# Output projections, norms and residual by tokens, in two staggered halves

## The chip, the cores and the metric

The kernel runs on one core of one Trainium2 chip. A core has five engines that run side by side, each through its own instructions in order: TensorE (PE; its weight loads are listed apart, as PEld), VectorE (DVE), ScalarE (ACT), GpSimd (POOL) and SyncE (SP), which here issues the transfers. They hand work to each other through semaphores. The metric is the device time of one execution in microseconds (us).

## The reference

Two layers over 256 latent tokens with 256 context tokens beside them, 1024 channels, float32. Each layer is a half-step feed-forward block, a token mixer, and a second half-step feed-forward block. In front of each stands a normalization with shift and scale, behind it a second one with a gate, and the result is added to the stream. The vectors for shift, scale and gate come from a conditioning vector times `w_mod`.

```python
def pre(x, m, k, g):
    return rms_norm(x, g) * (1 + m[:, 3 * k + 1, None]) + m[:, 3 * k, None]
def post(y, m, k, g):
    return m[:, 3 * k + 2, None] * rms_norm(y, g)
def swiglu(h, w_gu, w_down):
    gt, up = jnp.split(h @ w_gu, 2, axis=-1)
    return (jax.nn.silu(gt) * up) @ w_down
...
        x_lat = x_lat + FFN_RES * post(swiglu(pre(x_lat, m_lat, 0, g[0]), ff1_w_gu[i], ff1_w_down[i]), m_lat, 0, g[1])
```

`rms_norm` divides each token by the root of the mean square of its channels. The mixer of layer 0 is a gated depthwise convolution (31 taps) beside an attention with 8 heads, in which latent queries read a window of the latent grid and all context keys; that of layer 1 is a short gated convolution. The context is needed only up to the keys and values of layer 0. The feed-forward width is 2816.

## The kernel before

All activations lie with channels on the partitions and tokens along the free dimension: a stage's input is 8 tiles of 128 channels by 256 tokens (512 in ff1_0, where latent and context tokens run side by side). The stages follow one another: ff1_0, ev_in, ev_out, ff2_0 (layer 0), ff1_1, od_in, od_out, ff2_1 (layer 1).

Weights stream from memory in 162 chunks of 1 MB, each 16 tiles of 128x128, through SP's queue. A chunk is cut into four pieces of 128x512. ScalarE rounds a piece (`wh`, L190) and VectorE takes the rest (`wl`, L192); activations are split in the same way. Every product is three matmuls (`mm3`, L202 to L206): the weights are the stationary operand, the activations move, 256 columns at a time in the latent stages, 512 in ff1_0. Only the V projection (L624 to L626) has it the other way round.

A norm sums over channels, hence over partitions. `Post.tile` (L250) squares each output tile as it comes; `Post.rstd` (L266) sums over partitions by matmuls with a constant matrix (L271, L284), takes the power -1/2 on GpSimd (`power`, L214), and spreads the result over all partitions by matmuls with the identity (`spread`, L220). The mean square of the new stream is worked out from three sums, so that both powers need only one pass. Then `step` updates x (L308, L309) and builds the next input tile by tile (`pre_tile`, L226 to L237); the next stage's first matmuls run over its tiles for four output tiles at a time.

ff1_0 has four parts of 5, 5, 6 and 6 of the 22 hidden tiles; after each the down projection of that part is added up in `yp`. Products of `silu(c)` with `w_mod` run on VectorE as 1024-wide dot products (L126) in the background of ff1_0 and ff2_0; their rows are loaded as `mr` on SP's queue between the weights.

A scheduler sets the order of the instructions on each engine from the order of the program and the dependencies; the engines keep that order. Tile pools set how far ahead things may run: 3 weight chunks, 8 pieces of `wh` and of `wl`, and eight PSUM banks, four for products.

## Time and profile before

| | us |
|---|---|
| three runs | 1269.46, 1271.57, 1272.31 |
| median | 1271.57 |
| span of the profiled execution | 1270.2 |
| TensorE busy in it | 1228.3 (97%) |
| VectorE, ScalarE busy | 951.7 (75%), 632.8 (50%) |

The span runs from the first to the last instruction of one profiled execution. Busy time of TensorE counts matmuls from issue to modelled end, so the rate of a stream is read from the number of matmuls in a stretch, and a stop of the stream from the gap between two issues.

### The profile page before, as it was taken

How to read it: one execution, taken by the hardware profiler on the slowest of the kernel's cores; microseconds unless marked ns; L12 is line 12 of the kernel's file. 1: busy time of each engine (PE TensorE's matmuls, PEld its weight loads, DVE VectorE, ACT ScalarE, POOL GpSimd, SP SyncE). 2: the span in 40 equal slices, each digit the busy share in tenths (PEclk: the TensorE clock that was granted, in tenths of full speed). 3: DMA queues.
4: the chain of work that ended last, by engine and by line, in shares of the span. 5: the costliest groups of instructions: out<-in, count | busy, mean ns of one | idle time of the engine just before them, and what ended most of it. 6: DMA issues, size and time to landing. Idle time of an engine off the chain costs nothing.

```text
span 1270.2 us, 21721 instructions
## 1 busy us (share of the span) xinstructions
PE 1228.3 (97%) x8338; PEld 1125.4 (89%) x8338; DVE 951.7 (75%) x1919; ACT 632.8 (50%) x1262; POOL 16.6 (1%) x25
## 2 busy tenths in 40 slices
PE   7999999999999999989999999999998998999996
PEld 4688888888888986689999999999998998999996
DVE  4999998886358999877988868565667777755553
ACT  4543322322346746667555547555555555655551
POOL 0000000000000000000000000000000000000000
PEclk8999999999999999999999998999999998999998
DMA  8757788887221420126888944545453543554541
GB/s 305 298 198 268 285 309 324 296 295 277 100 83 50 167 100 34 67 100 229 350 320 331 348 180 138 195 174 192 177 188 118 189 176 116 202 196 170 196 167 34
DMA packets 37455, 252.22 MB, mean 199 GB/s; under 512 B 3940, under 2 KB 7140, under 8 KB 7144
## 3 DMA queue, kind: packets, MB, share of 16 engines
q1 hardware_dynamic: 37352, 250.85, 53.3%
q8 instruction: 65, 1.06, 0.3%
q14 instruction: 38, 0.31, 0.1%
HBM read 249.78 MB, written 1.05 MB: 197 GB/s over the span
## 4 chain that ended last, share of the span: by engine, by line
PE 85%; DVE 8%; DMA 3%; ACT 2%; issue 1%; POOL 1%; SPq 0%; POOLq 0%; DVEq 0%; ACTq 0%
PE mm L205 26%; PE mm L206 26%; PE mm L204 26%; DMA mr<-in_wmodb 2%; DVE bufD L567 2%; DVE junk L126 2%; DVE wl L192 1%; PE bc L668 1%; PE mm L647 1%; PE st L677 1%; DVE acc L262 1%; DMA xlc<-in_ctxT 1%; PE bc L220 1%; PE mm L625 0%; PE mm L626 0%
## 5 line engine op out<-in xcount | busy, mean ns | idle before, releaser
L190 ACT CAST wh<-wr 128x512 fp32r<-128x512 f32 x648 | 399.5, 622 | 467.0 <-PE mm L205 422.7
L192 DVE TENSOR_TENSOR wl<-wr,wh 128x512 fp32r<-128x512 f32 x648 | 442.0, 688 | 205.1 <-ACT wh L190 202.7
L205 PE MATMUL mm<-hin,wh 128*128 128x256 f32 x1248 | 355.4, 286 | 0.1
L206 PE MATMUL mm<-hin,wl 128*128 128x256 f32 x1248 | 355.2, 286 | 0.0
L204 PE MATMUL mm<-hin,wh 128*128 128x256 f32 x1248 | 350.7, 286 | 4.6 <-ACT hin L233 4.6
L204 PEld LDWEIGHTS mm<-hin,wh 128*128 128x128 f32 x1248 | 240.1, 195 | 5.5 <-ACT hin L233 5.5
L205 PEld LDWEIGHTS mm<-hin,wh 128*128 128x128 f32 x1248 | 243.3, 195 | 0.3 <-DVE hin L237 0.3
L206 PEld LDWEIGHTS mm<-hin,wl 128*128 128x128 f32 x1248 | 243.1, 195 | 0.0
L126 DVE SCALAR_TENSOR_TENSOR junk<-mr,cb 128x1024 bf16<-128x1024 f32 x156 | 190.3, 1220 | 8.9 <-DMA mr<-in_wmodb 8.2
L204 PE MATMUL mm<-hh,wh 128*128 128x512 f32 (+1 forms) x464 | 170.1, 371 | 2.0 <-ACT hh L427 1.3
L205 PE MATMUL mm<-hl,wh 128*128 128x512 f32 (+1 forms) x464 | 171.7, 371 | 0.0
L206 PE MATMUL mm<-hh,wl 128*128 128x512 f32 (+1 forms) x464 | 171.1, 370 | 0.4 <-DVE wl L192 0.4
L204 PEld LDWEIGHTS mm<-hh,wh 128*128 128x128 f32 x464 | 87.6, 190 | 17.6 <-ACT hh L427 1.8
L206 PEld LDWEIGHTS mm<-hh,wl 128*128 128x128 f32 x464 | 88.3, 190 | 15.2 <-DVE wl L192 0.8
L205 PEld LDWEIGHTS mm<-hl,wh 128*128 128x128 f32 x464 | 88.4, 190 | 14.8 <-DVE hl L237 0.2
L204 PE MATMUL mm<-Hc,wh 128*128 128x256 f32 x288 | 81.5, 283 | 0.0
L205 PE MATMUL mm<-Hd,wh 128*128 128x256 f32 x288 | 81.5, 283 | 0.0
L206 PE MATMUL mm<-Hc,wl 128*128 128x256 f32 x288 | 81.5, 283 | 0.0
L205 PE MATMUL mm<-Hl,wh 128*128 128x512 f32 (+1 forms) x182 | 69.8, 383 | 0.5 <-DVE Hl L326 0.5
L206 PE MATMUL mm<-Hh,wl 128*128 128x512 f32 (+1 forms) x182 | 69.5, 382 | 0.0
L204 PE MATMUL mm<-Hh,wh 128*128 128x512 f32 (+1 forms) x182 | 69.4, 382 | 0.0
L206 PEld LDWEIGHTS mm<-Hc,wl 128*128 128x128 f32 x288 | 55.2, 192 | 0.0
(217 smaller groups left out, 1701.9 us busy)
## 6 DMA issues: line engine op xcount, KB each, us to landing
wr<-in_wflow SPq DMA_DIRECT2D x162, 1024.0 KB, 4.8
mr<-in_wmodb SPq DMA_DIRECT2D x64, 1024.0 KB, 6.5
mr<-in_wmoda SPq DMA_DIRECT2D x4, 1024.0 KB, 8.7
wme<-in_wmoda SPq DMA_DIRECT2D x4, 1024.0 KB, 4.8
bt<-in_bias SPq DMA_DIRECT2D x2, 1024.0 KB, 5.6
xlc<-in_xT SPq DMA_DIRECT2D x2, 512.0 KB, 6.0
xlc<-in_ctxT SPq DMA_DIRECT2D x2, 512.0 KB, 8.1
out<-xlc SPq DMA_DIRECT2D x3, 256.0 KB, 2.6
```

The costliest lines, as they stand in the source:

```text
L126: nc.vector.scalar_tensor_tensor(junk, row, 1.0, cb[:, v, :], op0=ALU.mult, op1=ALU.mult, accum_out=mraw[:, l, v, ch, j:j + 1])
L190: nc.scalar.copy(h, r)
L192: nc.vector.tensor_sub(lo, r, h.bitcast(F32))
L204: nc.tensor.matmul(ps, lhsT=wh, rhs=xh, start=start, stop=False, skip_group_check=check)
L205: nc.tensor.matmul(ps, lhsT=wh, rhs=xlo, start=False, stop=False, skip_group_check=check)
L206: nc.tensor.matmul(ps, lhsT=wl, rhs=xh, start=False, stop=stop, skip_group_check=check)
L220: nc.tensor.matmul(bc[:, t * P:(t + 1) * P], lhsT=r[:, t:t + 1].to_broadcast([P, P]), rhs=ident, start=True, stop=True)
L262: nc.vector.tensor_add(self.acc, self.acc, s)
L567: nc.vector.scalar_tensor_tensor(acc[:, i, :], src, dwh[:, i, d:d + 1], acc[:, i, :], op0=ALU.mult, op1=ALU.add)
L647: nc.tensor.matmul(ps, lhsT=qT[rows, i, t * P:(t + 1) * P], rhs=kT[rows, i, :], start=True, stop=True)
L668: nc.tensor.matmul(pt[:, kt * P:(kt + 1) * P], lhsT=pr[:, kt * P:(kt + 1) * P], rhs=dg, start=True, stop=True)
L677: nc.tensor.matmul(po[m * DH:(m + 1) * DH, :S], lhsT=vv[:, kt, h * DH:(h + 1) * DH], rhs=pTs[:, m, kt, :], start=(kt == 0), stop=(kt == 3))
```

## The change

The output projections (FFN down, ev_out, od_out) now have the activations stationary and 512 weight columns moving (`rows3`), so that their outputs lie with tokens on the partitions: two token halves of 128, each in two banks of 512 channels. In `Out` all but the last four k-tiles run for both halves; the last four run first for half 0 and then for half 1. Each half has its own norm: `residual` squares on ScalarE with the sum along the row, multiplies by the gate, which now lies as a row on all partitions (`gate_row`, by way of memory on GpSimd's queue), takes the power on GpSimd, updates x, which now lies by tokens (`xt`), and squares x again for the second power. `turn` scales x, transposes it on TensorE (8 transposes of 128x128 a half) and applies shift and scale. The next FFN's first two hidden tiles (the head) are computed by tokens and by halves (`head_mm`) and transposed (`head_turn`); the other twenty stay as before. The 2 MB of x and context by tokens are loaded by an extra transfer. The weights come in halves of a chunk (5 buffers), with 12 pieces ahead; modulation rows in 512 KB, 4 buffers; six PSUM banks hold products. ff1_0 has five parts of 4, 4, 4, 5 and 5. The K projection runs as two times 256 columns. The output is stored by tokens.

```diff
-TAIL = ((0, 2), (2, 2), (4, 2), (6, 1), (7, 1))
+HEAD = 2
+TAIL = 4
...
-PARTS0 = (5, 5, 6, 6)
-BG0 = (4, 1)
+PARTS0 = (4, 4, 4, 5, 5)
+BG0 = (4, 2)
...
+RING = 12
+RAW = CHUNK // 2
...
+    def gate_row(l, v, k, res):
+        p = mod_post(l, v, k, res)
+        flat = dram.tile([KD, P], F32, name=f"prow{l}{v}{k}")
+        nc.gpsimd.dma_start(out=flat.rearrange("k p -> p k"), in_=p)
+        row = mraw_p.tile([P, D], F32, name="pr", tag="mr")
+        nc.gpsimd.dma_start(out=row, in_=flat.rearrange("k p -> (k p)").partition_broadcast(P))
+        return row
...
+    def load(n, m):
+        if (n, m) not in raws:
+            raws[n, m] = wraw.tile([P, RAW], F32, name="wr")
+            nc.sync.dma_start(out=raws[n, m], in_=wflow[n][:, m * RAW:(m + 1) * RAW])
+        return raws[n, m]
...
+    def rstd(ss):
+        u = small.tile([P, 1], F32, name="uu")
+        nc.vector.scalar_tensor_tensor(u, ss[:, 0:1], EPS, ss[:, 1:2], op0=ALU.add, op1=ALU.add)
+        r = small.tile([P, 1], F32, name="rr1")
+        nc.gpsimd.tensor_tensor(r, u, nhalf[:, :1], op=ALU.pow)
+        return r
+    def square(ss, n, y):
+        nc.scalar.activation(ajunk, y, AF.Square, scale=1.0 / 32, accum_out=ss[:, n:n + 1])
...
+    def residual(y, row, x, yw, out_t=None):
+        ss = small.tile([P, 2], F32, name="ss")
+        for n in range(2):
+            c = slice(n * 512, (n + 1) * 512)
+            square(ss, n, y[n])
+            nc.vector.tensor_mul(yw[:, c], y[n], row[:, c])
+        r = rstd(ss)
+        s2 = small.tile([P, 2], F32, name="s2")
+        for n in range(2):
+            c = slice(n * 512, (n + 1) * 512)
+            nc.vector.scalar_tensor_tensor(x[:, c], yw[:, c], r, x[:, c], op0=ALU.mult, op1=ALU.add)
+            if out_t is None:
+                square(s2, n, x[:, c])
+            else:
+                nc.sync.dma_start(out=out_t[:, c], in_=x[:, c])
+        return rstd(s2) if out_t is None else None
...
+    def turn(x, rx, xs, a, b, h, t):
+        ts = slice(t * P, (t + 1) * P)
+        for n in range(2):
+            c = slice(n * 512, (n + 1) * 512)
+            nc.scalar.activation(xs[:, c], x[:, c], AF.Copy, scale=rx)
+            pt = bank(ps_bc, "bc")
+            for q in range(4):
+                nc.tensor.transpose(pt[:, q * P:(q + 1) * P], xs[:, n * 512 + q * P:n * 512 + (q + 1) * P], ident)
+            full = work.tile([P, 512], F32, name="gh")
+            for q in range(4):
+                k = 4 * n + q
+                nc.vector.tensor_scalar(full[:, q * P:(q + 1) * P], pt[:, q * P:(q + 1) * P], a[:, k:k + 1],
+                                        b[:, k:k + 1], op0=ALU.mult, op1=ALU.add)
+            fv = full.rearrange("p (q t) -> p q t", t=P)
+            nc.scalar.copy(h[:, 0, 4 * n:4 * n + 4, ts], fv)
+            nc.vector.tensor_sub(h[:, 1, 4 * n:4 * n + 4, ts], fv, h[:, 0, 4 * n:4 * n + 4, ts].bitcast(F32))
...
+    def rows3(ps, src, k, ts, w, start, stop):
+        wh, wl = w
+        nc.tensor.matmul(ps, lhsT=src[:, 0, ts], rhs=wh, start=start, stop=False)
+        nc.tensor.matmul(ps, lhsT=src[:, 0, ts], rhs=wl, start=False, stop=False)
+        nc.tensor.matmul(ps, lhsT=src[:, 1, ts], rhs=wh, start=False, stop=stop)
...
+    class Out:
+        def __init__(self, name, base, src, K, row, final=False):
+            w = lambda k, n: wtile(name, base + k * KD + n * 4, 4)
+            y = [[bank(ps_mm, "mm") for _ in range(2)] for _ in range(2)]
+            tmp = big.tile([P, 4, D], F32, name="tmp", tag="E")
+            self.xs = [tmp[:, 2 + t, :] for t in range(2)]
+            self.rx = []
+            for k in range(K - TAIL):
+                for t in range(2):
+                    for n in range(2):
+                        rows3(y[t][n], src(k), k, TS[t], w(k, n), k == 0, False)
             for t in range(2):
...
+                for n in range(2):
+                    for k in range(K - TAIL, K):
+                        rows3(y[t][n], src(k), k, TS[t], w(k, n), False, k == K - 1)
+                self.rx.append(residual(y[t], row, xt[:, t, :], tmp[:, t, :], out[t] if final else None))
...
+    def half_step(prev, name, l, k, final=False, nbg=0):
+        a, b = mod_pre(l, 0, k)
+        hin = lat_in()
...
+        def head_mm(t):
+            ps = bank(ps_mm, "mm")
+            for kk in range(KD):
+                rows3(ps, hin[:, :, kk, :], kk, TS[t], wtile(name, 4 * kk, 4), kk == 0, kk == KD - 1)
...
+        prev.turn(0, a, b, hin)
+        head_mm(0)
+        prev.turn(1, a, b, hin)
+        head_mm(1)
...
+            if f == HEAD:
+                head_turn(0)
+                head_turn(1)
+            gate_up(H(f)[:, 0, :], H(f)[:, 1, :], ps[:, :S], ps[:, S:], S)
...
+        row = gate_row(l, 0, k, 0.5)
+        bg(nbg)
+        return Out(name, NF * 16, H, NF, row, final)
...
+    xt = big.tile([P, 4, D], F32, name="xt", tag="X")
+    nc.sync.dma_start(out=xt, in_=xtok)
...
+            def turn0(t):
+                turn(xt[:, t, :], rxs[t], yp[:, t, :], *pre[t // 2], hs[t // 2], t % 2)
+        for t in range(4):
+            ts = slice(t * P, (t + 1) * P)
+            y = [bank(ps_mm, "mm") for _ in range(2)]
+            for n in range(2):
                 for k in range(nf):
...
+                    wh, wl = wtile("ff1_0", base + k * KD + n * 4, 4)
+                    nc.tensor.matmul(y[n], lhsT=Hh0[:, k, ts], rhs=wh, start=k == 0, stop=False)
+                    nc.tensor.matmul(y[n], lhsT=Hh0[:, k, ts], rhs=wl, start=False, stop=False)
+                    nc.tensor.matmul(y[n], lhsT=Hl0[:, k, ts], rhs=wh, start=False, stop=k == nf - 1)
+            for n in range(2):
+                c = slice(n * 512, (n + 1) * 512)
+                if pi == 0:
+                    nc.scalar.copy(yp[:, t, c], y[n])
+                else:
+                    nc.vector.tensor_add(yp[:, t, c], y[n], yp[:, t, c])
+            if last:
+                rxs.append(residual([yp[:, t, :512], yp[:, t, 512:]], prow[t // 2], xt[:, t, :], yp[:, t, :]))
+                if t >= 2:
+                    turn0(t - 2)
...
+    turn0(2)
+    turn0(3)
...
+            for v in range(2):
+                mm3(ps[:, v * S:(v + 1) * S], wtile("ev_in", 128 + i * KD + k), hs[v][:, 0, k, :], hs[v][:, 1, k, :],
+                    k == 0 and v == 0, k == KD - 1, True)
...
+    post = Out("ev_out", 0, lambda k: mix[:, :, EV_ORDER[k], :], KD, gate_row(0, 0, 1, 1.0))
+    post = half_step(post, "ff2_0", 0, 2, nbg=BG1)
...
+    hin = lat_in()
+    post.turn(0, a, b, hin)
+    post.turn(1, a, b, hin)
```

In the fences below the order on one engine is shown, of the program before and of the one after, an instruction a row with its line, kind, output and inputs. First VectorE between ff2_0 and ff1_1. Before (L282 and L274 sums, L300 to L297 the small vectors of the norm, L308 and L309 the update of x, L226 the input):

```order
L282 TENSOR_TENSOR sq_7525<-sq_7525,acc 128x256
L274 TENSOR_SCALAR uu<-st 128x2
L282 TENSOR_TENSOR sq_7525<-sq_7525,acc 128x256
L300 COPY rc_7593<-rr 128x2
L288 COPY xy<-mm 128x2
L292 SCALAR_TENSOR_TENSOR q_7584<-st,rr,xy 128x1 x2
L295 SCALAR_TENSOR_TENSOR sx<-q_7584,rr,sx 128x1 x2
L308 TENSOR_TENSOR xn<-yg,bc 128x256
L297 TENSOR_SCALAR sx<-sx 128x2
L309 TENSOR_TENSOR xlc<-xlc,xn 128x256
L226 TENSOR_TENSOR xn<-xlc,bc 128x256
```

After (L243 the gate product, L229 the sum in front of a power, L248 the update of x, L267 shift and scale, L194 a weight split):

```order
L243 TENSOR_TENSOR tmp<-mm,pr 128x512 x2
L229 SCALAR_TENSOR_TENSOR uu<-ss 128x1
L194 TENSOR_TENSOR wl<-wr,wh 128x512
L248 SCALAR_TENSOR_TENSOR xt<-tmp,rr_7234,xt 128x512 x2
L194 TENSOR_TENSOR wl<-wr,wh 128x512 x3
L229 SCALAR_TENSOR_TENSOR uu<-s_7236 128x1
L194 TENSOR_TENSOR wl<-wr,wh 128x512 x2
L243 TENSOR_TENSOR tmp<-mm,pr 128x512 x2
L229 SCALAR_TENSOR_TENSOR uu<-ss 128x1
L267 TENSOR_SCALAR gh<-bc,a_7320,b_7321 128x128
L248 SCALAR_TENSOR_TENSOR xt<-tmp,rr_7276,xt 128x512 x2
L267 TENSOR_SCALAR gh<-bc,a_7320,b_7321 128x128 x3
```

The sums over partitions and small vectors are gone. The first gate product to the first update of x belong to half 0, the second L243 row and its updates to half 1; they stand within the shift and scale of half 0.

Next TensorE where attention ends and the out projection of the even mixer begins. Before (L668 and L677 attention, L204 to L206 the projection, L579 and L574 the convolution's norm):

```order
L574 MATMUL st<-bufD,bufE 128x256
L668 MATMUL bc<-bufE,gh 128x128 x4
L668 MATMUL bc<-bufE,gs 128x128 x4
L204 MATMUL mm<-mix,wh 128x256
L205 MATMUL mm<-mix,wh 128x256
L206 MATMUL mm<-mix,wl 128x256
L204 MATMUL mm<-mix,wh 128x256
```

After (L677 and L686 attention, L590, L602 and L585 the convolution's norm, L276 to L278 the projection):

```order
L585 MATMUL mm<-bufD,bufE 128x256
L677 MATMUL bc<-bufE,gh 128x128 x2
L677 MATMUL bc<-bufE,gs 128x128 x3
L590 MATMUL mm<-bufE,xn 128x128 x2
L677 MATMUL bc<-bufE,gs 128x128
L602 MATMUL mm<-ident,full 128x128 x2
L686 MATMUL mm<-bufE,bufD 64x256 x8
L276 MATMUL mm<-wh,mix 128x512
L277 MATMUL mm<-wl,mix 128x512
```

The projection's first matmul stood between two units of the attention; now it stands behind the last.

Last SP's queue early in ff1_0 (`wr` weights, `mr` and `wme` modulation rows). Before:

```order
L381 DMA wme<-in_wmoda 128x2048
L181 DMA wr<-in_wflow 128x2048
L138 DMA mr<-in_wmodb 128x2048 x2
L181 DMA wr<-in_wflow 128x2048 x3
L138 DMA mr<-in_wmodb 128x2048 x2
L181 DMA wr<-in_wflow 128x2048
```

After:

```order
L386 DMA wme<-in_wmoda 128x2048
L185 DMA wr<-in_wflow 128x1024 x3
L134 DMA mr<-in_wmodb 128x1024 x4
L185 DMA wr<-in_wflow 128x1024
L479 DMA xt<-in_xtok 128x4096
L134 DMA mr<-in_wmodb 128x1024
L185 DMA wr<-in_wflow 128x1024
```

The load of the tokens (`xt`) has come between weight loads; the loads behind it are issued after it.

## Rows read from the trace of the kernel before

**Rows 1.** The page: engine totals, chain that ended last, landing of weight loads.

```profile
PE 1228.3 (97%) x8338; PEld 1125.4 (89%) x8338; DVE 951.7 (75%) x1919; ACT 632.8 (50%) x1262; POOL 16.6 (1%) x25
...
PE 85%; DVE 8%; DMA 3%; ACT 2%; issue 1%; POOL 1%; SPq 0%; POOLq 0%; DVEq 0%; ACTq 0%
...
wr<-in_wflow SPq DMA_DIRECT2D x162, 1024.0 KB, 4.8
```

**Rows 2.** Busy time by stretch: us, engine busy (instructions) in PE, PEld, DVE, ACT, POOL order.

```profile
1075.00:1255.00 180.00, 180.00 (x1503) 180.00 (x1502) 106.29 (x190) 96.22 (x188) 0.00 (x0) 1.00 0.46 166
...
280.00:370.00 90.00, 90.00 (x399) 74.53 (x398) 46.97 (x77) 27.53 (x46) 0.00 (x0) 1.00 0.49 173
```

**Rows 3.** Timeline of PE in the V projection: start, duration, line, operands.

```profile
459.63 0.39 PE L626 MATMUL mm<-wh,hl 128*128 128x512 f32 x1
...
462.80 0.39 PE L625 MATMUL mm<-wl,hh 128*128 128x512 f32 x1
```

**Rows 4.** Timeline of all engines in the norm between ff2_0 and ff1_1.

```profile
757.36 0.28 PE L206 MATMUL mm<-Hf,wl 128*128 128x256 f32 x1
...
759.46 0.74 POOL L214 TENSOR_TENSOR rr<-uu,nhalf 128x2 f32<-128x2 f32 x1 [195.55 <-DVE uu L274]
...
761.94 0.77 POOL L214 TENSOR_TENSOR rr<-sx,nhalf 128x2 f32<-128x2 f32 x1 [1.74 <-DVE sx L297]
...
762.76 0.71 PE L220 MATMUL bc<-ident,rr 128*128 128x128 f32 x4 [1.53 <-POOL rr L214]
...
763.97 0.60 ACT L233 ACTIVATE hin<-xn,b,a 128x256 fp32r<-128x256 f32 x1 [5.17 <-DVE xn L226]
...
764.62 1.22 PE L204 MATMUL mm<-hin,wh 128*128 128x256 f32 x4 [1.15 <-ACT hin L233]
```

**Rows 5.** Timeline of PE in the norm between od_out and ff2_1.

```profile
1058.45 0.28 PE L206 MATMUL mm<-mixo,wl 128*128 128x256 f32 x1
...
1066.03 1.22 PE L204 MATMUL mm<-hin,wh 128*128 128x256 f32 x4 [1.15 <-ACT hin L233]
```

**Rows 6.** Busy time by stretch in and behind the norm of rows 4; granted clock is PEclk.

```profile
757.50:764.60 7.10, 3.85 (x26) 2.92 (x24) 4.07 (x17) 1.75 (x6) 1.51 (x2) 0.94 0.00 1
764.60:770.50 5.90, 5.88 (x27) 5.88 (x28) 5.72 (x14) 4.39 (x13) 0.00 (x0) 0.50 0.00 0
```

**Rows 7.** Groups by line and shape: count, busy us, mean ns of one.

```profile
L192 DVE TENSOR_TENSOR wl<-wr,wh 128x512 fp32r<-128x512 f32 x648 | 442.0, 688 | 205.1 <-ACT wh L190 202.7
L190 ACT CAST wh<-wr 128x512 fp32r<-128x512 f32 x648 | 399.5, 622 | 467.0 <-PE mm L205 422.7 <-ACT gs L322 23.6 <-issue 8.0
...
L567 DVE SCALAR_TENSOR_TENSOR bufD<-av,dwh,bufD 128x256 f32<-128x256 f32 x120 | 52.0, 476 | 0.0
...
L324 DVE TENSOR_TENSOR gh<-gs,mm 128x512 f32<-128x512 f32 x21 | 14.4, 686 | 13.7 <-PE mm L206 13.5
...
L656 ACT ACTIVATE gh<-mm,nm 128x512 f32<-128x512 f32 x8 | 5.5, 685 | 2.6 <-DVE nm L653 2.6
```

**Rows 8.** Timeline of all engines at the end of the program.

```profile
1258.13 0.28 PE L206 MATMUL mm<-Hf,wl 128*128 128x256 f32 x1
...
1266.38 0.42 DVE L767 TENSOR_TENSOR xlc<-xlc,gs 128x256 f32<-128x256 f32 x1
```

**Rows 9.** Timeline of PE between ff1_0 and ev_in.

```profile
397.73 0.28 PE L206 MATMUL mm<-Hh,wl 128*128 128x256 f32 x1
...
407.14 0.74 PE L204 MATMUL mm<-hh,wh 128*128 128x256 f32 x4 [0.70 <-ACT hh L233]
```

**Rows 10.** Busy time by stretch in the even mixer (columns as in rows 2).

```profile
433.00:465.00 32.00, 31.39 (x180) 27.62 (x179) 30.69 (x78) 18.07 (x37) 0.77 (x1) 1.00 0.27 100
488.00:500.00 12.00, 10.74 (x60) 6.44 (x58) 11.36 (x47) 9.61 (x24) 1.01 (x1) 1.00 0.00 1
```

**Rows 11.** Busy time by stretch in ff1_0 (columns as in rows 2).

```profile
75.00:225.00 150.00, 149.64 (x660) 123.26 (x659) 138.77 (x247) 48.51 (x81) 0.00 (x0) 1.00 0.76 287
```

**Rows 12.** Waits of 60 to 380 us: engine, line, waited for, us, times, longest.

```profile
DVE junk L126 <- DMA mr<-in_wmodb: 7.4, 10, 1.6
```

371 lines of the change are left out of this document (110 added, 261 removed).

## The prediction

> **What bounds the kernel now.** I read the engine totals and the chain of waits first [rows 1]: TensorE is busy 97% of the span and 85% of the chain that ended last is its own work, so time goes only where the matmul stream is shortened or where it stops. Next the rate of that stream [rows 2]: with 256 moving columns 1503 matmuls go in 180.00 us, 0.1198 us each; with 512 columns 399 in 90.00 us, 0.2256 each. The V projection already runs as the change wants it, activations stationary and 512 weight columns moving; fifteen matmuls from 459.63 to 462.80 are 14 steps of 0.2264 us [rows 3].
>
> Then the stops. In the norm between ff2_0 and ff1_1 [rows 4] the last matmul of the stream issues at 757.36 and the next at 764.62, 7.26 us later: squares on ScalarE, a power on GpSimd (759.46), a second one (761.94), the spread over the partitions, the first input tile on ScalarE at 763.97. There are four such norms between latent stages; the longest, after od_out, has 7.58 us [rows 5]. I take 7.3. Behind it TensorE goes on at half the granted clock: from 764.60 to 770.50 the granted clock is 0.50, the lower of its two levels (1.2 GHz), after the stop [rows 6]. Two more stops are of another kind: 9.41 us between ff1_0 and ev_in [rows 9], and the end, 1258.13 to the end of the span at 1270.2 [rows 8].
>
> **The streaming term.** Counted in the two programs, 2100 matmuls with 256 columns leave and 1050 with 512 come: each FFN's down projection gives up 528, its first two head tiles 96; the out projections the rest, and the K projection, now split over two inputs, takes some back. 2100 x 0.1198 = 251.6 us go, 1050 x 0.2264 = 237.7 come: **-13.9 us**. With 0.2256 for the wide ones it would be -14.7. I take the row of V, whose operands stand the same way round.
>
> The Trainium skill (TensorE: Matmul & The Clock Gate, section "Back-to-back issue gap") states N/2.4 + 2.5 ns for a warm matmul. Two narrow ones would then cost 2.5 ns more than one wide one, 1050 times 2.6 us, and the sum below would end near 1283. The rows here show 13.2 ns (2 x 119.8 - 226.4), so the trace disagrees and the rows decide.
>
> **The norms between stages.** Before, all 256 tokens meet the norm at once. After, the last 24 matmuls of token half 0 run ahead of the last 24 of half 1, so half 0's norm has 24 x 0.2256 = 5.4 us of cover. But its chain is longer than the old one. I followed it by the new order on each engine, with durations of [rows 7]; zero is the issue of half 0's last matmul.
> The square of 512 columns with its sum takes 0.69 + hand-off, ends at 0.96. The gate product on VectorE (0.69) reads the same bank and waits for it: 1.69. Sum 1.77, power on GpSimd 0.74 as in [rows 4]: 2.65. Two updates of x, 512 columns each: no such row, between 0.69 (plain product) and 0.95 (twice the 256-column form, 0.476); I take 0.75 as nearer to the plain one: 3.45 and 4.23. Second squares 5.45, sum 6.1, second power 7.0. Scaled copies on ScalarE (0.62 as a cast, 0.1 more for the scale, an estimate) 7.76 and, behind a square of half 1, 9.04. The transposes follow, but VectorE's order puts half 1's gate product, sum and both x updates (ready only after the third power, 10.1) ahead of three of the four products that make the first input tiles. They end at 12.3, the cast (0.62) at 13.0. First head matmul: 13.0, that is 7.6 us after half 1's last matmul at 5.4.
> Then TensorE has the head tiles of half 0, 5.4 us, but two transposes of half 1 stand third in its order and wait for the fourth power and copy, until 14.6 (1.1 us lost), and half 1's inputs are ready near 22.5 while half 0's head ends at 19.6 (2.8 lost). Together 7.6 + 1.1 + 2.8 = 11.5 us against 7.3: **+4.2** at each of the three FFN boundaries, 12.6. Before the short-convolution mixer there is no head by halves; both halves must be there, first matmul at 17.5, 12.1 lost against 7.3: **+4.8**. The bounds for one boundary: if the cover works fully, 13.0 - 5.4 and nothing behind it, 7.6, or no change; if the weight splits queued in between (0.69 each on VectorE, four of them there) all land on the path, 14.3, or +7.
>
> The half clock: its stretch in [rows 6] holds 27 matmuls in 5.90 us, which at 0.1198 would be 3.2; up to 2.7 us are lost there, part of it the wait for input tiles. A longer stop can put another half stretch into each; I take +0.5 at four places, **+2.0**, bounds 0 and +6.
>
> **The other places.** ff1_0 to ev_in: half 0 to 3 of the two streams turn one after another in the last part; the first ev_in matmul needs tokens 0 to 255 and has two token halves of context behind it as cover; I get 6.5 to 7 us of stop plus 16 transposes in the stream, 1.9 at the rate of 256 columns, against 9.41 [rows 9]: **0**, bounds -3 and +3. The end: one power instead of one power and the spread; squares, product, sum, power, two x updates end 4.7 us after the last matmul, then as before 3.4 us from the end of the last update (1266.8) to the end [rows 8]: 8.1 against 12.1: **-4.0**.
> The even mixer: VectorE is full there, 30.69 of 32 us and 11.36 of 12 [rows 10], so its relief counts. The context's norm (8 tiles of five 256-column operations and their sums, about 12 us) leaves for 5.6 us of two turns; against it the out projection no longer fills TensorE's waits within the attention, since its first matmul now stands behind all of it; TensorE is idle 1.3 us of the 12 in 488 to 500 as it stands. Net **-1**, bounds -5 and +4.
> ff1_0: five parts instead of four, so 8 more additions of 512 columns, 8 x 0.69 = 5.5 us on a VectorE that is busy 138.8 of 150 us [rows 11]; TensorE loses 0.4 us there now. And a 2 MB load of the tokens by rows goes through SP's queue ahead of weight and modulation loads, at 287 GB/s 7 us. It waits until the last modulation tile is used; by then 12 weight tiles of the head stage are open and 8 beyond them are buffered, 20 x 3 x 0.2264 = 13.6 us of cover. **+1**, bounds -1 and +7. The gate rows go through memory on GpSimd's queue, long before their use; GpSimd has no work for 195 us ahead of a norm [rows 4], so I cost them at nothing; without that cover it is two landings, up to 4.8 us each [rows 1].
>
> **The sum.** -13.9 + 12.6 + 4.8 + 2.0 + 0 - 4.0 - 1 + 1 = **+1.5**. It stands against the profiled execution, whose span is 1270.2 us; the runs shown have 1269.46 to 1272.31, median 1271.57, 1.4 above that span, and what lies around the span is not touched. The span gives 1271.7, the median 1273.1; I take **1272.5**, between them: the shorter stream is paid back at the norms.
>
> **Rivals.**
> Even, as summed, 1268 to 1277: 0.41.
> The stagger covers: half 1's work hides half 0's norm, the splits and updates of half 1 slip behind half 0's inputs, and the loss per boundary stays at 7.3. Then the 17.4 us of the norms drop to 0 to 6 and the time is 1255 to 1261, say 1258. For it: VectorE has 4.07 us of work in 7.10 of the old stop [rows 6]; against it, the fixed order of the engines' queues. 0.26.
> A slower one at the same place: on VectorE a weight split stands between half 0's sum and its first x update, and on ScalarE casts stand between the squares. If the weight transfer of that split has not landed at 1.9 us, the whole chain waits behind it, half a landing to a whole one (4.8 us, [rows 1]) at four boundaries, +10 to +19; with the even sum's other terms 1284. It decides from the point where the split's input lands later than the power (2.65). Against it: in the old stop the DMA share is 0.00, the buffers had been filled before. 0.14.
> The token load: if it holds the weights beyond the 13.6 us of cover, a stop of 5 to 8 us arises near 60 us into the run: 1279. For it: transfers run at 287 GB/s a little later and VectorE already waits for modulation rows [rows 11, 12]. 0.13.
> The wide matmuls give nothing (0.2396 each or more, by which the stream is no shorter): 1286. Against it both rates are rows of this kernel [rows 2, 3]. 0.06. The Trainium skill's rule above would end at 1283.
>
> **How the numbers follow.** A measurement of this kernel can tell about 0.2%, 2.5 us, from no change: 1269.0 to 1274.1. The even case has 0.24 within it, 0.06 below, 0.11 above. Faster: 0.26 + 0.06 = 0.32. Same: 0.24. Slower: 0.11 + 0.14 + 0.13 + 0.06 = 0.44. The range reaches to the middle of the fast case and to the slow one at the norms, 1258 to 1284; the even case alone 1268 to 1277.
>
> **What would show it.** Right: wide matmuls every 0.226 us in the down projections; about 13 us from half 0's last matmul to the first head matmul, with three products of half 0 behind the x updates of half 1; the od_in stop near 12; about 8 us after the last matmul. Wrong: a stop after half 1's last matmul of 3 us or less (the cover works), one above 10 (something queued ahead waits), a stop between 50 and 75 us, or TensorE idle for over 6 us in the attention.

## Result and profile after

The changed kernel takes 1337.73 us (median of 4 runs, 1333.59 to 1340.38) against 1271.94 for the kernel before, a ratio of 1.052 (95% interval 1.0496 to 1.0543). The forecast was 1272.5, its range 1258 to 1284: 65 us were missed. The profiled execution of the changed kernel took 1333.59 us, its span 1331.7, that is 61.5 over the 1270.2 of before.

The page of the changed kernel: engine totals, transfers, the chain that ended last, and the group of the modulation's dot products; then that group in the kernel before.

```profile
PE 1226.6 (92%) x7240; PEld 1069.4 (80%) x7240; DVE 909.2 (68%) x1762; ACT 589.7 (44%) x1143; POOL 35.4 (3%) x52
...
DMA packets 71703, 257.90 MB, mean 194 GB/s; under 512 B 7988, under 2 KB 10164, under 8 KB 70968
...
PE 66%; DVE 11%; issue 10%; DMA 9%; ACT 2%; POOL 1%; SPq 0%; DVEq 0%; POOLq 0%; ACTq 0%
...
L124 DVE SCALAR_TENSOR_TENSOR junk<-mr,cb 128x1024 bf16<-128x1024 f32 x156 | 190.7, 1222 | 77.7 <-DMA mr<-in_wmodb 77.1
```

```profile
L126 DVE SCALAR_TENSOR_TENSOR junk<-mr,cb 128x1024 bf16<-128x1024 f32 x156 | 190.3, 1220 | 8.9 <-DMA mr<-in_wmodb 8.2
```

Against [rows 1]: TensorE's busy time is only 1.7 us shorter, as more of it runs at the lower granted clock (the mean over the span is 0.956 of full speed, 0.983 before; in a_best below it is 0.979, and the busy time 1212.1), and its share fell from 97% to 92%, so it stands more. DMA went from 3% of the chain to 9%: VectorE now waits 77.1 us for rows of the modulation matrix, 8.2 before.

Where the 61.5 us lie, from first matmul to first matmul of the stages (us, timelines of TensorE). Beside them stand four kernels of the experiments below:

| stage | before | after | a_release | a_pools | a_row | a_best |
|---|---|---|---|---|---|---|
| ff1_0 | 383.8 | 422.2 | 396.6 | 415.4 | 391.6 | 385.1 |
| even mixer | 158.7 | 172.8 | 173.8 | 160.8 | 172.4 | 159.6 |
| ff2_0 | 198.8 | 206.9 | 206.7 | 220.9 | 203.7 | 202.0 |
| ff1_1 | 199.8 | 204.1 | 205.5 | 206.6 | 207.7 | 205.0 |
| odd mixer | 101.6 | 101.0 | 100.6 | 100.8 | 100.7 | 100.7 |
| ff2_1 and end | 204.2 | 201.3 | 200.9 | 201.1 | 202.6 | 201.5 |

The parts on which most of the forecast's working went came nearly as said. TensorE in the norm between ff2_0 and ff1_1 (start, duration, line, operands; half 0's last matmul, half 1's, the first head matmul, the end of the next stop), the counterpart of [rows 4]:

```profile
811.46 0.40 PE L278 MATMUL mm<-wh,Hf 128*128 128x512 f32 x1
...
816.99 0.40 PE L278 MATMUL mm<-wh,Hf 128*128 128x512 f32 x1
...
825.30 0.79 PE L276 MATMUL mm<-wh,hin 128*128 128x512 f32 x1 [3.24 <-ACT hin L270]
...
835.05 0.44 PE L349 MATMUL bc<-ident,gh 128*128 128x128 f32 x2 [1.55 <-DVE gh L267]
```

From 811.46 to 825.30 are 13.84 us (forecast 13.0), to 835.05 23.6 (forecast 22.5 for half 1's inputs, whose first matmul comes 0.65 us later). The wide stream and the end, counterparts of [rows 2] and [rows 8]: 54.00 us hold 239 matmuls, 0.2259 us each, and the span ends at 1331.7, 7.2 us after the last matmul (forecast 8.1).

```profile
1268.00:1322.00 54.00, 54.00 (x239) 44.61 (x238) 23.43 (x36) 20.36 (x35) 0.54 (x1) 1.00 0.34 115
...
1324.53 0.40 PE L278 MATMUL mm<-wh,Hf 128*128 128x512 f32 x1
```

So the miss is mostly in ff1_0 (+38.4) and the even mixer (+14.1), which the forecast had at +1 and -1.

### The profile page after: what moved, and what is told of

The parts are those of the page before. It is cut to its first block, busy times and chain, and to the rows that moved or that the text cites. A ratio compares the mean times of both kernels' runs of the same rounds, so it can differ in the third digit from the quotient of the medians.

```text
span 1331.7 us, 19607 instructions
## 1 busy us (share of the span) xinstructions
PE 1226.6 (92%) x7240; PEld 1069.4 (80%) x7240; DVE 909.2 (68%) x1762; ACT 589.7 (44%) x1143; POOL 35.4 (3%) x52
## 4 chain that ended last, share of the span: by engine, by line
PE 66%; DVE 11%; issue 10%; DMA 9%; ACT 2%; POOL 1%; SPq 0%; DVEq 0%; POOLq 0%; ACTq 0%
PE mm L206 13%; PE mm L208 13%; PE mm L207 13%; DMA mr<-in_wmodb 8%; PE mm L276 6%; PE mm L278 6%; PE mm L277 6%; DVE junk L124 4%; PE mm L515 2%; PE mm L516 2%; PE mm L517 2%; DVE wl L194 2%; POOL rr L231 1%; DVE xt L248 1%; DVE gh L267 1%
## 5 line engine op out<-in xcount | busy, mean ns | idle before, releaser
L194 DVE TENSOR_TENSOR wl<-wr,wh 128x512 fp32r<-128x512 f32 x648 | 436.9, 690 | 219.3 <-ACT wh L192 218.7
L206 PE MATMUL mm<-hin,wh 128*128 128x256 f32 x1152 | 327.3, 284 | 1.9 <-ACT hin L270 1.9
L207 PE MATMUL mm<-hin,wh 128*128 128x256 f32 x1152 | 327.3, 284 | 0.0
L124 DVE SCALAR_TENSOR_TENSOR junk<-mr,cb 128x1024 bf16<-128x1024 f32 x156 | 190.7, 1222 | 77.7 <-DMA mr<-in_wmodb 77.1
L206 PEld LDWEIGHTS mm<-hin,wh 128*128 128x128 f32 x1152 | 221.9, 193 | 2.4 <-ACT hin L270 2.3
L207 PEld LDWEIGHTS mm<-hin,wh 128*128 128x128 f32 x1152 | 222.1, 193 | 0.3
L206 PE MATMUL mm<-hh,wh 128*128 128x512 f32 x352 | 138.4, 395 | 1.3 <-ACT hh L438 1.3
L208 PE MATMUL mm<-hh,wl 128*128 128x512 f32 x352 | 138.1, 393 | 0.8 <-DVE wl L194 0.8
L207 PE MATMUL mm<-hl,wh 128*128 128x512 f32 x352 | 138.1, 392 | 0.0
L515 PE MATMUL mm<-wh,Hh 128*128 128x512 f32 x176 | 70.5, 404 | 35.8 <-ACT Hh L311 34.2
L206 PEld LDWEIGHTS mm<-hh,wh 128*128 128x128 f32 x352 | 66.6, 190 | 15.7 <-ACT hh L438 1.8
L207 PEld LDWEIGHTS mm<-hl,wh 128*128 128x128 f32 x352 | 66.8, 190 | 13.9
L517 PE MATMUL mm<-wh,Hl 128*128 128x512 f32 x176 | 70.2, 400 | 1.4 <-DVE Hl L312 1.4
L516 PE MATMUL mm<-wl,Hh 128*128 128x512 f32 x176 | 69.7, 398 | 0.0
L578 DVE SCALAR_TENSOR_TENSOR bufD<-av,dwh,bufD 128x256 f32<-128x256 f32 x120 | 49.8, 472 | 0.0
L310 DVE TENSOR_TENSOR gh<-gs,mm 128x256 f32<-128x256 f32 (+1 forms) x82 | 39.9, 486 | 8.8 <-PE mm L208 8.0
```

The source lines that it names most:

```text
L124: nc.vector.scalar_tensor_tensor(junk, row, 1.0, cb[:, v, :], op0=ALU.mult, op1=ALU.mult, accum_out=mraw[:, l, v, ch, j:j + 1])
L194: nc.vector.tensor_sub(lo, r, h.bitcast(F32))
L206: nc.tensor.matmul(ps, lhsT=wh, rhs=xh, start=start, stop=False, skip_group_check=check)
L207: nc.tensor.matmul(ps, lhsT=wh, rhs=xlo, start=False, stop=False, skip_group_check=check)
L208: nc.tensor.matmul(ps, lhsT=wl, rhs=xh, start=False, stop=stop, skip_group_check=check)
L515: nc.tensor.matmul(y[n], lhsT=Hh0[:, k, ts], rhs=wh, start=k == 0, stop=False)
```

## Experiments: what holds up the first FFN

The down projection of ff1_0 loops token tile, output half, block, so each split piece is kept until the last of four token tiles. In the changed kernel ScalarE's weight casts wait long for a matmul (L517) to give a piece back (waits of ScalarE from 140 to 360 us; tile and line, waited for: us in total, times, longest):

```profile
ACT Hh L311 <- DVE gh L310: 76.5, 10, 15.4
ACT wh L192 <- PE mm L517: 53.1, 3, 20.2
```

In the second row it waits 53.1 us in three waits. Theory H: the held pieces make the stops. Rivals: the modulation rows on SP's queue (M), the token load (X).

**a_release**: pieces used by all four token tiles at once, then given back (weights packed to match).

```
-  for t in range(4): for n in range(2): for k in range(nf): ...
+  for n in range(2): for k in range(nf): for t in range(4): ...   # not in the last part
```

> The changed kernel with one edit in ff1_0: in the down projection of every part but the last the loop over the four token tiles goes inside the loop over hidden tiles (column half outermost, weights packed in that order), so that a weight piece is used four times in a row and released, where before the edit all 8 to 10 pieces of a part were held until the last token tile. Same matmuls, same loads, same dot products. Theory H (held pieces: ScalarE's casts stand 16 to 20 us in each down phase, VectorE's splits and the dot products queued behind them stand too, and the backlog stops TensorE at the end of the next part): the stops of 21 and 14 us near 212 and 317 us shrink below 3 us together, ff1_0 from 422 to about 388 us, the time to about 1302. Theory M (the modulation rows, loaded in 512 KB pieces through SP's queue, come late and VectorE waits for them): the stops stay, 1330 to 1338.

1309.04 us (ratio to the kernel before 1.031, 95% interval 1.0284 to 1.0336; below, brackets give this interval alone). That is 28.7 less than the changed kernel, 25.6 of it in ff1_0. Two stops of 8 us stayed, near 213 and 303. H explains a part.

**a_mrpool**: the modulation rows on GpSimd's queue.

```
-  nc.sync.dma_start(out=cur, in_=wmodb[n])
+  nc.gpsimd.dma_start(out=cur, in_=wmodb[n])
```

> The changed kernel with the modulation rows of the background dot products loaded through GpSimd's queue instead of SP's, so that they are no longer queued between weight loads, nor the weight loads behind them. Theory M: VectorE's 77 us of waits for these rows fall below 20 and the time falls by 25 to 35 us, to about 1305. Theory H: the casts still stand for held pieces in the down phases, the waits of the splits stay, and the time moves by less than 10 us, to 1328 to 1338.

1338.57 us (1.0513 to 1.0574), and VectorE still waits 53.5 us for the rows: M falls.

**a_latext**: the 2 MB load of the tokens set, in the program, in front of the last part of ff1_0 instead of behind the head stage.

```
-nc.sync.dma_start(out=xt, in_=xtok)      # behind the head stage
+if pi == len(parts) - 1: nc.sync.dma_start(out=xt, in_=xtok)
```

> The changed kernel with the 2 MB load of the tokens by rows issued in front of the last part of ff1_0 instead of in front of the first. Theory X (that load, ahead of weights and modulation rows in SP's queue near 60 us, starts the delay): the time falls by 7 us or more, to 1330 or less, and the waits of VectorE for modulation rows up to 168 us shrink. Theory H: within 3 us of the changed kernel, 1335 to 1340.

1326.85 us (1.0421 to 1.048): 10.9 less, 7.5 in ff1_0, though no stop had stood between 50 and 75 us. The load did not move far: the scheduler still sets it early on SP's queue, 7 us later than in the changed kernel (timelines of SP, the changed kernel first).

```profile
56.46 0.33 SPq L479 DMA_DIRECT2D xt<-in_xtok  x1
```

```profile
63.47 0.42 SPq L483 DMA_DIRECT2D xt<-in_xtok  x1
```

What these 7 us spare was not told apart.

**a_rel_xt**: both.

> The changed kernel with the two edits of the first study together: weight pieces of ff1_0's down phases released as they are used (alone 1309.0, 28.7 us faster than the changed kernel), and the load of the tokens by rows put in front of the last part (alone 1326.9, 10.9 faster). If both take away parts of one backlog on VectorE and what is left of it is small: the two stops of 8 us that the first edit left are gone and the time is 1290 to 1296. If the token load only shifted the phase between loads and dot products, which the release has changed too: nothing more, 1305 to 1310. If they add up: 1298.

1303.53 us (1.0219 to 1.0303), in none of the three ranges; the two stops remain. **a_dots**: fewer dot products in ff1_0, more in ff2_0.

```
-BG0 = (4, 2); BG1 = 1
+BG0 = (3, 2); BG1 = 2
```

> The changed kernel with fewer background dot products in ff1_0 (3 instead of 4 behind each hidden tile, so 98 instead of 120 in all) and the rest in ff2_0 (2 a step instead of 1). The pieces are held as in the changed kernel. Theory H with a full VectorE (a part of 65 us has some 55 us of work there, so that waits above 11 us a part become a backlog): with 5 us less work a part the backlog shrinks, ff1_0 loses 15 us or less instead of 36, and the time is 1312 to 1322 if ff2_0 takes the dot products in its idle time. If the waits themselves make the stops, whatever the load: 1333 to 1340.

1317.4 us (1.031 to 1.0417): ff1_0 falls to 388.8, by 33.4; ff2_0 and ff1_1 pay 11.6 and 8.2 of it back.

**b_half**: the kernel before with each load in two halves, as the change has them. (In this expectation and those of a_pair, a_all and a_best the "early" token load is the one of a_latext, which is issued some 7 us later than in the changed kernel.)

```
-  wraw bufs=3, tiles of CHUNK; mraw bufs=2, tiles of CHUNK
+  wraw bufs=6, tiles of CHUNK // 2; mraw bufs=4, tiles of D
```

> The kernel before with one thing of the change: every load of weights and of modulation rows in two halves (512 KB, 4 KB to a partition, in twice as many buffers of half the size), projections and norms untouched. Theory W (size of the transfers): in the stretch 100 to 300 us the kernel before moves 302 GB/s at 80% of the DMA engines, the changed kernel with released pieces and early token load 278 GB/s at 90%, so a megabyte in halves costs a quarter more engine time, loads come late and the dots that wait for them hold up VectorE; the first FFN grows by 6 to 20 us, 1278 to 1292 us. Rival N (the size does not matter while the total is the same, the loss is in the by-token loops alone): 1269 to 1275 us.

1279.73 us (1.0049 to 1.0102): +9.3 over the kernel before, in its profile 6.1 in ff1_0 (waits of 5.4 and 3.7 us of TensorE, close together) and 4.2 in ff2_0; VectorE waits 46.0 us for modulation rows instead of 8.2. The size of the loads costs something by itself. **a_pair** gives a_rel_xt the modulation rows in 1024 KB again.

```
-cur = mraw_p.tile([P, D], ...);      nc.sync.dma_start(out=cur, in_=wmodb[n])
+cur = mraw_p.tile([P, CHUNK], ...);  nc.sync.dma_start(out=cur, in_=wmodb[n // 2])   # two buffers
```

> The changed kernel with pieces released in the first FFN and the token load early (1303.5 us), and the modulation rows and the position bias again loaded 1024 KB at a time into two buffers, as in the kernel before; the weights stay in halves. Theory W (size of the transfers): the two stops left in the first FFN, some 10 us each near 213 and 303 us, shrink by half or more, 1285 to 1295 us. Rival N: 1300 to 1307 us, or slower by the coarser buffers.

1311.15 us (1.0298 to 1.0365), 7.6 slower, ff1_0 the same (395.8 against 395.5): the two stops do not come from the rows' size. **a_all** put everything found until then together, with four parts and dots spread into ff1_1.

```
-PARTS0 = (4, 4, 4, 5, 5); BG0 = (4, 2)
+PARTS0 = (6, 6, 5, 5); BG0 = (3, 1); half_step(post, "ff1_1", 1, 0, nbg=2)
 and a_rel_xt, a_pools (below), a_pair
```

> The changed kernel with all that the runs so far point to: pieces released in the first FFN, four parts instead of five (6, 6, 5, 5), token load early, the mixer's banks in pools as before, modulation rows in 1024 KB loads, and fewer dots in the first FFN (3 behind a block instead of 4), the rest spread into the third FFN. If the first FFN's +38 and the mixer's +14 are load and order alone, both nearly go and what stays is the four norms' +15 to +20 less streaming 14 and end 4: 1272 to 1285 us. Rival (the by-token form itself costs the first FFN and the mixer): 1295 us or more.

1304.87 us (1.0246 to 1.0301). The rival's number came, but not for its reason, as the next runs show: some 15 us are still lost near 200.

What every one of these kernels kept shows when the transfers are laid beside the stops. In the changed kernel GpSimd issues the write of a gate vector (L168), VectorE then waits for modulation rows, and TensorE stands 13.74 us for a product of the SwiGLU that is queued on VectorE behind them (timelines of POOL, DVE and PE):

```profile
307.82 0.88 POOL L168 DMA_DIRECT2D prow<-p  x1 [66.75 <-DVE p L161]
...
320.53 1.23 DVE L124 SCALAR_TENSOR_TENSOR junk<-mr,cb 128x1024 bf16<-128x1024 f32 x1 [6.82 <-DMA mr<-in_wmodb]
...
327.99 1.23 DVE L124 SCALAR_TENSOR_TENSOR junk<-mr,cb 128x1024 bf16<-128x1024 f32 x1 [5.01 <-DMA mr<-in_wmodb]
...
330.52 0.80 PE L515 MATMUL mm<-wh,Hh 128*128 128x512 f32 x1 [13.74 <-ACT Hh L311]
```

The same stretch in 7 us windows (PE, PEld, DVE, ACT, POOL busy, granted clock, DMA share, GB/s):

```profile
303.00:310.00 7.00, 7.00 (x32) 5.80 (x31) 5.85 (x13) 0.62 (x1) 0.88 (x1) 1.00 0.96 315
310.00:317.00 7.00, 6.79 (x30) 5.27 (x29) 3.56 (x6) 3.29 (x6) 0.00 (x0) 1.00 0.85 153
317.00:324.00 7.00, 0.00 (x0) 0.00 (x0) 2.44 (x4) 0.00 (x0) 0.00 (x0) 0.72 0.69 79
324.00:331.00 7.00, 0.48 (x1) 0.48 (x2) 3.01 (x6) 0.62 (x1) 0.00 (x0) 0.50 0.92 352
```

Behind the write the transfers fall from 315 to 79 GB/s while the DMA engines stay 0.69 to 0.85 busy: they are not idle, they carry little. (The share counts a transfer's whole time in the window in which it starts, so it can pass 1.) The vector lies as 8 values on each of 128 partitions and is written transposed, 1024 values of 4 bytes, each to its own place in memory. Five of the seven such writes fall into ff1_0 (146, 151, 191, 240, 308 us), because the scheduler sets them as early as their vectors are ready. Theory G: the write stops the loads.

**b_scatter**: the kernel before with only these writes added; nothing reads them.

```
 p = ... mod_post ...
+flat = dram.tile([KD, P], F32, ...)
+nc.gpsimd.dma_start(out=flat.rearrange("k p -> p k"), in_=p)
```

> The kernel before, which does the same work, plus the seven writes of gate vectors to memory that the changed kernel makes (128 partitions x 8 values, written transposed: 1024 pieces of 4 bytes, on GpSimd's queue); nothing reads them. Five fall into the first FFN. In the changed kernel with released pieces the DMA engines move 10 to 70 GB/s instead of 350 for about 8 us, some 6 to 7 us behind each such write, at full busy share. Theory G (the write itself stops the loads): the first FFN of the kernel before also gets stops, 1280 to 1305 us. Rival (the dips come from the changed kernel's own demand, the write is harmless): 1268 to 1274 us.

1287.83 us (1.0107 to 1.0156): +17.2, 15.0 of it in ff1_0, with loops, pieces and loads of before. Its longest stop (POOL and PE timelines, then windows):

```profile
168.16 0.88 POOL L168 DMA_DIRECT2D prow<-p  x1 [46.85 <-DVE p L166]
...
182.27 0.80 PE L207 MATMUL mm<-Hh,wh 128*128 128x512 f32 x1 [9.21 <-ACT Hh L328]
```

```profile
160.00:167.00 7.00, 7.00 (x33) 5.79 (x31) 6.57 (x12) 0.56 (x2) 0.00 (x0) 1.00 1.04 407
167.00:174.00 7.00, 6.05 (x27) 4.69 (x25) 4.43 (x10) 2.72 (x6) 0.88 (x1) 1.00 1.19 176
174.00:181.00 7.00, 0.00 (x0) 0.00 (x0) 3.02 (x6) 0.00 (x0) 0.00 (x0) 0.64 0.58 51
181.00:188.00 7.00, 5.73 (x16) 4.32 (x17) 5.22 (x8) 1.76 (x3) 0.00 (x0) 0.63 0.91 379
...
244.00:251.00 7.00, 7.00 (x32) 5.81 (x31) 3.38 (x6) 2.89 (x5) 0.00 (x0) 1.00 0.29 37
```

407 GB/s, the write at 168.16, then 51 and a stop of 9.2 us. The last row shows another dip, to 37 GB/s behind the write at 238.04, that TensorE does not feel. That what a dip costs depends on how much is buffered when it comes is my reading; the buffers were not counted.

The packets tell the kernels apart. Of those of 4 KB or more on SP's queue (median 0.16 us, or 0.31 where loads are of 1024 KB), 41 take over 3 us in the changed kernel and 59 in b_scatter, up to 8.9 and 8.7 us, and every one starts between the issue and the landing of such a write. In the kernel before, b_half, a_row and a_best there is none. The write itself is recorded as 16 packets of 256 bytes; why load packets take so long beside them the traces do not say.

**a_row**: the changed kernel with the vector turned on TensorE first and written as 8 rows of 512 bytes; the writes also move to where the turning matmul stands, 377 us and later.

```
-nc.gpsimd.dma_start(out=flat.rearrange("k p -> p k"), in_=p)
+nc.tensor.matmul(pt[0:KD, :P], lhsT=p, rhs=ident, start=True, stop=True)
+nc.scalar.copy(pc, pt[0:KD, :P])
+nc.gpsimd.dma_start(out=flat, in_=pc)
```

> The changed kernel with one thing else: the gate vector is turned on TensorE (one matmul of 128 columns against the identity), copied, and written as 8 rows of 512 bytes, so memory gets 8 pieces instead of 1024. Loops, held pieces, order of loads as in the changed kernel. Theory G: the first FFN falls from 422 us by 20 to 38, 1298 to 1318 us. Rival H (the held weight pieces are the cause, the write only finds them): 1328 to 1340 us.

1302.56 us (1.0219 to 1.0269): 35.2 less, 30.6 of it in ff1_0; held pieces, token load and half-size loads are all still there. How much of this is the form of the write and how much its later place was not told apart. Time from issue to landing over the run, of the changed kernel and of a_row, and VectorE's waits of 60 to 415 us in both:

```profile
prow<-p POOLq DMA_DIRECT2D x7, 4.0 KB, 12.5
```

```profile
prow<-full POOLq DMA_DIRECT2D x7, 4.0 KB, 3.8
```

```profile
DVE junk L124 <- DMA mr<-in_wmodb: 49.4, 18, 7.7
```

```profile
DVE junk L124 <- DMA mr<-in_wmodb: 16.0, 11, 3.2
```

The Trainium skill (DMA: Bandwidth & Descriptors, section "Specifications") asks for at least 512 bytes in a transfer for full rate and says that smaller ones cost a read-modify-write; its section "Queues, rings and completion order" says that an engine drains a whole packet of one queue before it turns to another. That small pieces are slow agrees here, 12.5 us against 3.8 to land; the read-modify-write and the turn of an engine are seen in no run. The price is the traces' own: for some 10 us other transfers go at 16 to 116 GB/s (windows of 2 us from 312 to 322) or 25 to 75 (b_scatter, 170 to 180).

## Experiments: the mixer, the norms, the end

**b_evorder**: the kernel before with the blocks of ev_out in an order in which none of them can run within the attention.

```
-EV_ORDER = (0, 1, 2, 4, 5, 6, 3, 7)
+EV_ORDER = (7, 3, 0, 1, 2, 4, 5, 6)
```

> The kernel before with the order in which the even mixer's out projection takes its inputs changed: the two that the attention and the convolution finish last come first, so that none of its matmuls can run between those of the attention. Theory F (the filling was worth what the even mixer lost in the changed kernel, 14 us more than before): 1280 to 1285. Rival (VectorE's own work sets the end of the attention, filled or not, and the matmuls only move): within 3 us of before, 1270 to 1275.

1274.58 us (1.0025 to 1.0054), +4.5; in its profile the mixer is 6.0 longer and ff1_0 2.3 shorter. The filling that the change gives up is worth that and no more.

In the changed kernel the convolution's norm stands in front of the first scores (TensorE's timeline):

```profile
528.37 0.60 PE L585 MATMUL mm<-bufD,bufE 128*128 128x256 f32 x2
530.55 0.71 PE L590 MATMUL mm<-bufE,xn 128*128 128x128 f32 x4 [1.58 <-ACT xn L588]
533.11 1.22 PE L602 MATMUL mm<-ident,full 128*128 128x128 f32 x4 [1.85 <-DVE full L598]
534.26 3.79 PE L656 MATMUL mm<-bufC 64*128 64x512 f32 x8
```

Before, the first scores follow directly on the norm's first product:

```profile
487.73 0.59 PE L574 MATMUL st<-bufD,bufE 128*128 128x256 f32 x2
488.26 1.13 PE L647 MATMUL mm<-bufC 64*128 64x512 f32 x4
```

The change gave all six banks to one pool, so scores, convolution norm and outputs take turns in one ring. **a_pools** goes back to four and two.

```
-ps_mm bufs=6
+ps_mm bufs=4; ps_st bufs=2   # ps_st: convolution norm, attention output, third head pair of ff1_0
```

> The changed kernel with the PSUM banks divided as in the kernel before, four for products and two apart, the latter for the convolution's norm, the attention's outputs and the heads. Theory P (with six banks in one pool the scheduler put the first convolution norm's matmuls, which wait for ScalarE, VectorE and GpSimd in turn, ahead of the first scores; in the order of this variant they stand between scores as in the kernel before): the 3.4 us of stops in front of the scores go and the attention runs 4 to 8 us shorter, 1329 to 1334. Rival (the even mixer is longer because its out projection fills nothing any more, worth 4.5 us in the first study): within 2 us of the changed kernel.

1332.76 us (1.043 to 1.0538). The mixer gives back 12.0 of its 14.1 us; the scores take 34.2 us from first to last instead of 42.3 (35.2 before). All of it is lost again in ff2_0 (+14.0): TensorE stands twice for 6.3 us, near 738 and 746, for a product queued on VectorE behind waits for modulation rows. VectorE waits 28.3 us for these rows in that stage and 27.7 in the changed kernel, so these waits are not longer in sum but fall elsewhere; why was not told apart. ff1_0 is 6.8 shorter in this run, so that the total came inside the expected range by luck. In a_best, without the transposed writes, the mixer's gain stays.

**a_tail1**: the halves staggered by one block of the down projection instead of four, 1.4 us of cover for half 0 instead of 5.4.

```
-TAIL = 4
+TAIL = 1
```

> The changed kernel with a stagger of one k-tile instead of four: half 1 has 6 matmuls of its own behind half 0's last one, 1.4 us instead of 5.5. If the stagger covers what it was worked out to cover, each of the four norms between latent stages stops TensorE 4.1 us longer: +16, 1352 to 1356. If VectorE's order (half 1's products and updates ahead of three products of half 0) and the transposes of half 1 early in TensorE's order take the cover back, the time moves by less than 6 us, 1332 to 1344.

1339.49 us (1.0483 to 1.059), 1.8 more, as if the stagger hid almost nothing. The stages say otherwise: ff1_0, whose matmuls the edit does not touch, is 5.1 shorter in this run, and ff2_0, ff1_1 and the odd mixer together are 12.8 longer. In the norm between ff2_0 and ff1_1 TensorE now stands 10.75 us from half 1's last matmul to the first head matmul, 8.31 in the changed kernel (first and last row; the counterpart of 816.99 to 825.30).

```profile
813.77 0.40 PE L278 MATMUL mm<-wh,Hf 128*128 128x512 f32 x1
819.41 2.30 PE L263 MATMUL bc<-ident,tmp 128*128 128x128 f32 x8 [5.25 <-ACT tmp L260]
824.52 0.79 PE L276 MATMUL mm<-wh,hin 128*128 128x512 f32 x1 [2.81 <-ACT hin L270]
```

Summed over the four norms, TensorE loses some 11 us more than in the changed kernel, where 16 was worked out for a full cover. So the stagger hides about two thirds of what it was meant to.

**a_order**: half 1's residual set behind half 0's shift and scale.

```
-self.rx.append(residual(y[t], row, ...))
+res = lambda t=t: self.rx.append(residual(y[t], row, ...))   # half 1: called first thing in turn(1)
```

> The changed kernel with the second token half's residual written behind the first half's shift and scale, so that VectorE and ScalarE finish half 0's chain before they begin half 1's; at the end of the kernel nothing is changed. Theory C (half 1's chain ends last, what half 0 gains half 1 loses): within 4 us of 1337.7. Rival D (half 0's chain is held up by half 1's instructions): 2 to 3 us less at each of three FFN norms and the mixers' two, 1323 to 1331 us.

1324.73 us (1.0388 to 1.0477). At the three norms in front of an FFN the stop is 6.5 to 6.6 us instead of 8.3 to 8.4 (first row below, from 806.60), in front of the odd mixer 16.7 instead of 12.4, since both halves must be turned there (TensorE's timeline).

```profile
813.12 0.79 PE L276 MATMUL mm<-wh,hin 128*128 128x512 f32 x1 [1.95 <-ACT hin L270]
...
1018.66 1.97 PE L263 MATMUL bc<-ident,tmp 128*128 128x128 f32 x8 [9.55 <-ACT tmp L260]
```

These stops sum to -1; of the 10.6 us between the two profiles 7.9 are in ff1_0, which the edit does not touch. So it was tried again with the four edits that gained something in their stage. **a_best**: a_rel_xt with the banks of a_pools and the gate rows of a_row.

> The changed kernel with released pieces, early token load, the mixer's banks in pools as before, and gate vectors written by rows: all four causes that the runs point to. Theory G with the others: the first FFN within 4 us of the kernel before's 383.7, the mixer some 5 us shorter than in the changed kernel, the second FFN some 4 us shorter: 1278 to 1292 us. Rival (the stops stay): 1296 us or more, as with released pieces, early load and pools alone.

1280.85 us (1.0054 to 1.0113): 56.9 of the 66 us are gone, ff1_0 and the mixer stand within 1.4 us of before. Of the 7.7 us that its profile is over that of before (1270.2), the norms give about +22.8 (counted below), streaming -13.9, the end -5.0; 3.8 are scattered. **a_best2** adds a_order's change at the three FFN norms alone.

> The kernel with all four causes taken out (1280.9 us), and the second half's residual behind the first half's shift and scale at the three norms in front of an FFN alone; in front of the odd mixer, where both halves are turned before anything multiplies, it stays as it was (there the later residual cost 4 us in the run before). Theory D: 1.5 to 2.5 us at each of three norms, 1273 to 1277 us. Rival C (the second half pays it back): 1279 to 1283 us.

1276.93 us (1.0036 to 1.007): inside the range of theory D, though its ratio and a_best's are not clearly apart. **a_best3** loads weights in 1024 KB again.

```
-RING = 12; RAW = CHUNK // 2; wraw bufs=5
+RING = 11; RAW = CHUNK; wraw bufs=3
```

> The same with the weights loaded 1024 KB at a time into three buffers, as in the kernel before (the ring of split pieces goes from 12 to 11 to make room; the modulation rows stay in 512 KB). Theory W: the halved loads cost the kernel before 9 us, most of it by the weights, so 3 to 8 us less than the run beside it, 1266 to 1273 us. Rival N (in this kernel no load ends last any more): within 2 us of the run beside it.

1275.59 us (1.0033 to 1.0069), as a_best2: with the stops gone the size of the loads costs nothing that shows here.

The form, with all that could be mended, is still about 0.5% slower than the kernel before. It pays where no norm follows. **b_final**: the kernel before with only ff2_1's down projection by tokens.

```
+rows3(t, n, k): activations of half t stationary, 512 weight columns moving; last 4 blocks half by half
+to_tokens(): 16 transposes of x during gate and up;  gate_row(); residual by tokens; out by tokens
```

> The kernel before with only the last FFN's down projection by tokens (512 weight columns moving, the last four blocks token half by token half, rows of the gate through memory, the residual's input transposed on TensorE during the gate and up projections), so neither a norm in front of another sublayer nor the first FFN is touched. By the measured pieces: streaming -3.4 (528 matmuls at 119.8 ns against 264 at 226.4 ns), end -4 to -5 (12.1 against 7.2 us after the last matmul), 16 transposes +1: 1264 to 1267 us, faster than both. Rival: the four banks and eight held pieces at the turn to the down projection cost 3 us or more, 1268 to 1273 us.

1264.31 us against 1270.39 (12 and 17 runs, ratio 0.9956, 0.9938 to 0.9974): 0.4% faster than the kernel before. Its last stage takes 198.0 us instead of 204.2; the last matmul stands at 1257.11 and the span ends at 1264.3.

```profile
1257.11 0.40 PE L372 MATMUL mm<-wh,Hf 128*128 128x512 f32 x1
```

## Why the prediction was wrong

**Streaming, -13.9: right.** 0.2259 us for a wide matmul as [rows 3] said; b_final shows the exchange alone, 59.8 us of down projection instead of 63.1. (The formula of the Trainium skill that the prediction sets against these rows is given in the section it names for an isolated matmul, a case that this stream does not show.)

**ff1_0, +1: the step that failed most, 38 us.** Its sentence "The gate rows go through memory on GpSimd's queue, long before their use; ... so I cost them at nothing" asked when the row is needed and never what its write does to the transfers of others. b_scatter shows the harm alone (+17.2 in a kernel with more slack), a_row the gain (-35.2, with the later place of the writes in it). A second step failed in the same place: the prediction counted buffers where the token load comes and not for the new loop order, by which one part holds 8 to 10 of the 12 pieces (a_release, -28.7, in which the writes of ff1_0 also fall at other times, 165 to 287 us). The two do not add, 30.6 and 25.6 in ff1_0 are more than the 38.4 there are. My reading, argued and not shown: a dip of some 10 us becomes a longer stop because the pieces that would bridge it are held, and either remedy takes most of it. [rows 11] showed VectorE at 138.8 of 150 us and the DMA share at 0.76, so there was little room for either; I read it as a bound on eight additions.

**The token load, a rival at 1279: its place was wrong.** No stop stood at 50 to 75 us; the load issued 7 us later gains 10.9 all the same, and why is open.

**Even mixer, -1: failed by 14** (1.1 of the stage's 14.1 is the norm at its end, counted below). The lost filling was named and is 4.5 us (b_evorder). The pools were not: the order rows of one pool instead of two put a norm's three products in front of the scores (a_pools, -12.0 there). With that put right, and the filling still lost, a_best's mixer is 0.9 us over before, so the balance that the prediction drew was near.

**Norms, +17.4 with +2.0 for the clock: the mechanism right, the size a quarter short.** Summed over the gaps between issues beyond the rates above, the four norms lose about 14.9, 12.5, 13.1 and 15.1 us against 7.2, 8.3, 7.7 and 8.2: +24 instead of +19.4 (a_best +23). The chain is 13.84 us for 13.0, and it starts 5.5 us before half 1 ends, as worked out.

**ff1_0 to ev_in, 0, and the end, -4.0: right.** The stop is 6.7 us (6.5 to 7), the end 7.2 (8.1) against 12.1.

**The other rivals.** That the stagger covers the norm fell with these sums; part of it it does cover, 2.4 us at the norm at 814 (a_tail1). The late weight split did not come: in the norm at 811 the x update waits for GpSimd's power (0.46 us, at 814.49), not for the split in front of it. The rest of the sum was near the truth: a_best, with ff1_0 and the mixer put right, is 1280.85, inside the range of 1258 to 1284 and 0.8% slower than before.

Open stay what the later token load spares and why a_pools lost in ff2_0 what it gained in the mixer. The terms above leave some 5 us of the 61.5; some 3 of them are waits within the stream of ff2_0 (4.8 us there, 1.9 before).
